# One Transformer layer on one core: the second token block's last products ahead of new weights at two norms, and two of four quads scaled on VectorE

## The chip, the core and the metric

The kernel runs on one core of one Trainium2 chip. The time is the device time of one execution in microseconds (us), the median of several. The engines are named as in the profile: PE is TensorE's matrix multiplication and PEld its weight load, DVE is VectorE, ACT is ScalarE, POOL is GpSimd and SP is SyncE, whose queue issues most loads. All of them work at once, each in the order of its own queue, and wait for one another by semaphores.

## What is computed

One decoder layer for 256 tokens of width 2048 in float32: a half-step SwiGLU feed-forward network (ffn 1), a norm, a mixer of two attention branches, a norm, a second feed-forward network (ffn 2) and a last norm. Cut to what matters here:

```python
def _layer_norm(x, g, b):
    mu = jnp.mean(xf, axis=-1, keepdims=True)
    var = jnp.mean(jnp.square(xf - mu), axis=-1, keepdims=True)
    return (xf - mu) * lax.rsqrt(var + LN_EPS) * g + b

def _swiglu(x, w_gate, w_up, w_down):
    return (jax.nn.silu(x @ w_gate) * (x @ w_up)) @ w_down

h = _layer_norm(ALPHA * h + 0.5 * _swiglu(h, ffn1...), ln1_g, ln1_b)
mix = _mixer(h, ...)          # starts with h @ w_in, ends with y @ w_out
h = _layer_norm(ALPHA * h + mix, ln2_g, ln2_b)
h = _layer_norm(ALPHA * h + 0.5 * _swiglu(h, ffn2...), ln3_g, ln3_b)
```

The two norms in the middle, ln1 and ln2, are the "inner" ones: each needs whole rows of what was just multiplied, and everything after it needs its result.

## The kernel before

**Precision.** Each float32 operand is held as two fp32r tiles, a rounded one and the rest: `split` (L151) casts on ScalarE (L152, the high part) and subtracts on VectorE (L153, the low part). `triple` (L204) then makes three matmuls of 512 columns out of one product (L205 to L207). Weights are loaded by SP into `raw` buffers (four of them), split into one of a ring of pairs (`wring`), and used. The activations are held the same way in `Acts`, as 16 tiles of 128 channels in four quads for each of two token blocks of 128 tokens. `Acts.put` (L137) splits one quad; `made[q, b]` is that quad's subtraction on VectorE.

**Order.** Work is traced in units. One unit is 256 rows of a weight: a load, a split (`prep`), the products of the first token block and those of the second. `project` (L209) goes over the units of one weight matrix. With a lag, the products of the second block are kept in the deque `behind` and run only when more than `lag[0]` units wait there (`catch_up`, L166). Around the inner norms `widen` (L926) sets the lag to 5 and the ring to 10 pairs. So at the end of a stage the first block's products end five units ahead of the second's; the first block's norm is to be computed while the second's products still run, and the second block's while the next weights meet the first block. In the traced order, the held units of the old stage stand between the first units of the new weights. What is traced is then ordered for each engine at build time, by what is ready and by place in the trace. `tc.issue_after(ins)` adds an order: what its block traces on the engine of `ins` comes behind `ins` in that engine's queue, without waiting for it to end.

**A norm.** `LayerNorm.evac` (L739) adds a finished bank to the residual rows `z` (L749, L751) and takes statistics (L754, L760). With the last bank of a block comes `apply` (L764): aggregate (L766), `rstd` (L657: two small VectorE operations, a root on ScalarE at L661, three small VectorE operations), and then for each of the four quads a scaling of the rows (L784) and `rows_to_quad` (L644). The latter turns 128 x 512 on TensorE by four transposes into one of three `tr` banks (L647), has ScalarE apply the gain and the bias of each channel in four activations of 128 columns (L652), and gives the result to `Acts.put`. Later, `finish` (L788) applies gain and bias to the rows as well (L790, L791), for the next residual, and writes them from POOL's queue (L1322). `later(n, fn)` holds such a step until n more units have run.

**The places.** `ffn` (L796) ends with the down projection in `Sliced.run` and `look(0, 0)` (L918). `mixer` (L1037) begins with `project(a["wc0"], ...)` (L1079), followed by wc1 and wc2 of 256 and 320 columns. After `w_out`, `ffn` 2 begins with `project(wgu[0], ...)` (L857), where `behind_x=3` queues the split's VectorE part of unit 3 and later behind `made[0, 0]`. After that come groups of seven products in place of eight (`Hybrid`, L340), in the mixer for two gate matrices (three groups) and for dq, dk and dv; the flag `small` marks the mixer's. At the end of a group, two additions close the second weight's banks (L450, L451), in the mixer all of them queued behind the newest split traced so far (`behind_split`, L333). `dqT` and `dkT` then go through VectorE, a write and a read of DRAM by POOL's queue, and a copy on ScalarE (L704) before the scores (L1156).

Of the kernel before, what the change touches and what calls it, by code (L numbers as in the profile page):

```python
# [18 lines left out]
P = 128  # L19
# [40 lines left out]
def layer_kernel(ctx: ExitStack, tc: tile.TileContext, a: dict, out: bass.AP):  # L60
# [55 lines left out]
    class Acts:  # L116
        def __init__(self, k, name, kept=()):
            self.name = name
            self.kept = kept
            self.tiles = {}  # L120
            self.ready = set()
            self.made = {}
            self.raws = {}

# [12 lines left out]
        def put(self, q, b, src, i0=0, n=4):  # L137
            hi, lo = self.quad(q, b)
            hi, lo = hi[:, i0:i0 + n, :], lo[:, i0:i0 + n, :]
            if len(src.shape) == 4:  # L140
                hi, lo = (v.rearrange("p k (i c) -> p k i c", i=4) for v in (hi, lo))
            self.made[q, b] = split(hi, lo, src)
            self.ready.update((4 * q + i0 + i, b) for i in range(n))

# [63 lines left out]

    def project(w, x, k_tiles, width, done, k0=0, hook=None, between=None, behind_x=None):  # L209
        banks = [None, None]  # L210
# [14 lines left out]
        def one(j):  # L225
# [8 lines left out]
            def prep():  # L234
                pair = [t[:, :G * width] for t in next_pair()]
                with tc.issue_after(x.made[0, 0].ins) if behind_x is not None and j >= behind_x else nullcontext():
                    for c in parts:
                        split(*(t[:, c] for t in pair), st["raw"][:, c])
                st["pair"] = [t.rearrange("p (g n) -> p g n", g=G) for t in pair]
# [100 lines left out]
    class Hybrid:  # L340
# [14 lines left out]

        def group(self, w0, w1, done, wide=False, seeded=False):
            banks = {}
# [68 lines left out]
            def plain(n, j, last=False):  # L426
# [13 lines left out]
                def now():  # L440
                    wh, wl = st["pair"]
                    for b in range(2):
                        o, first = bank(names[b])
                        for g in range(G):
                            k = 2 * j + g
                            triple(o, self.x.at(0, k, b), self.x.at(1, k, b), wh[:, g, :], wl[:, g, :],
                                   first and g == 0, last and g == 1, n == 1 or seeded)
                    if last:
                        with behind_split(1) if small else nullcontext():
                            done(1, 0, banks["Z"], n2, ALU.add)  # L450
                            done(1, 1, banks["X"], q5, ALU.add)  # L451
# [192 lines left out]
    def rows_to_quad(src, b, x, q, gain=None, shift=None):  # L644
# [3 lines left out]
        if gain is not None:  # L648
            full = x.raw(q, b) if q in x.kept else tmp_tile([P, 512], "full")
            for i in range(4):  # L650
                k = 4 * q + i
                S.activation(full[:, i * P:(i + 1) * P], t[:, i * P:(i + 1) * P], AF.Identity,  # L652
                             bias=shift[:, k:k + 1], scale=gain[:, k:k + 1])
            t = full
        x.put(q, b, t.rearrange("p (i t) -> p i t", i=4))

    def rstd(v, eps, n, between=None):  # L657
        ve = sm(n, "ve")
        V.tensor_scalar(out=ve, in0=v, scalar1=eps, scalar2=None, op0=ALU.add)
        sd = sm(n, "sd")  # L660
        S.activation(sd, ve, AF.Sqrt, scale=4.0)  # L661
        w = sm(n, "w")
# [43 lines left out]
    class LayerNorm:  # L706
        def __init__(self, scale, residual, g, bt, each, x=None, cols=None, at=((0, 2, 4, 6), (8, 11, 14, 17)), root_at=1):
# [11 lines left out]
            self.gb = [[None, None] for _ in range(2)]  # L719
            self.applied = {}  # L720

            def rows(h, b):
# [41 lines left out]
        def apply(self, b):  # L764
# [5 lines left out]
            if self.cols is None:  # L770
# [10 lines left out]
                return  # L781
            r = rstd(mv[:, 1:2], LN_EPS, 1)
            for c in range(4):
# [11 lines left out]

    def ffn(n, x, wgu, wdn, residual, g, bt, each, first=None, between=None, nxt=None, cols=None):  # L796
        hb = {}
# [53 lines left out]
        def first_hook(j):  # L851
            if first is not None:
                first(j)
            if j == 5:
                for i, f in enumerate([extra.make] + seven.steps):
                    later(2 * i + 1 - (i > 0), f)
        project(wgu[0], x, KD, 512, lambda b, bank: gu_done(0, b, bank), hook=first_hook,  # L857
                between=between, behind_x=3 if n == 2 else None)
        project(wgu[1], x, KD, 512, lambda b, bank: gu_done(1, b, bank), hook=second)
        look(3, 4)  # L860
# [21 lines left out]
        for p in range(2):  # L882
# [30 lines left out]
            else:  # L913
# [3 lines left out]
                     lambda m, b, bank, p=p: ln.evac(2 * p + m, b, bank), calls, 8 * p)  # L917
        look(0, 0)  # L918

    def at_unit(u, fn):  # L920
# [115 lines left out]

    def mixer(x):  # L1037
        c_row = [act_tile([P, 1024], F32, "c_row") for _ in range(2)]
# [39 lines left out]

        project(a["wc0"], x, KD, 512, cq_done)  # L1079
        narrow_to(6)  # L1080
# [28 lines left out]
        for i, f in ((0, 0), (1, 0), (0, 2)):  # L1109
            w = (a["wgm"], a["wgd"])[i]  # L1110
            hy.group(w[f], w[f + 1], lambda n, b, bank, snap, op, i=i, f=f: keep_gate(i, f + n, b, bank, snap, op),
                     False, f == 2)

# [210 lines left out]

    h1 = Acts(KD, "h1", (0, 1))
    ffn(1, xq, a["gu1"], a["dn1"], a["x"], a["ln1_g"], a["ln1_b"], keep(0), first_tokens, second_tokens, h1, a["ln1_cols"])

    yq = mixer(h1)
    h2 = Acts(KD, "h2", (0, 1, 2))
    ln = LayerNorm(1.0, res[0], a["ln2_g"], a["ln2_b"], keep(1), h2, a["ln2_cols"])  # L1330
    for c in range(4):
        project(a["w_out"][c], yq, KD, 512, lambda b, bank, c=c: ln.evac(c, b, bank),
                hook=at_unit(0, widen) if c == 3 else None)

    ffn(2, h2, a["gu2"], a["dn2"], res[1], a["ln3_g"], a["ln3_b"],
        lambda b, c, z: nc.sync.dma_start(out[b * P:(b + 1) * P, c * 512:(c + 1) * 512], z))
    catch_up(0)
# [84 lines left out]
```

## Time and profile before

| what | value |
| --- | --- |
| time, median of three runs | 1982.71 us (1981.73 to 1983.70) |
| the profiled execution, time | 1981.89 us |
| its span in the profile | 1979.8 us |
| TensorE's mean granted clock in it | 0.999 of full speed |
| DMA | 484.63 MB, mean 245 GB/s |

The span is the part of the time that the profile covers; 2.1 us lie outside it. Times in the listings are microseconds from the start of the span. A row of the order of time has the start, the time until the end of the last of the instructions merged in it, the engine, the line, what is written and what is read, and in square brackets how long the engine had sat idle before and what ended that. `mm` and `tr` are PSUM banks, `h` the split activations, `y` the mixer's result, `z` a norm's rows. Matmuls overlap, so a row of 0.39 us does not mean that the next can start only then.

### The profile page before, as it was taken

To read this page: it belongs to the slowest core of one execution; us is meant where nothing else is said; L and a number is where in the kernel's file an instruction comes from. 1 tells how busy PE (TensorE), PEld (TensorE's weight loads), DVE (VectorE), ACT (ScalarE), POOL (GpSimd) and SP (SyncE) were. 2 spreads that over 40 slices of the span, in tenths; PEclk is the share of its full clock that TensorE was granted. 3 is DMA by queue.
4 is the path that set the end of the run, shared out by engine and by line. 5 is a ranking of instruction groups with operands and counts; after the bars stand their busy time and mean duration, and the time that the engine had idled before them with its cause. 6 is when DMAs were issued, how large, how long until landed. Compare 5 with 4: busy or idle time off the path is not lost.

```text
span 1979.8 us, 25620 instructions
## 1 busy us (share of the span) xinstructions
PE 1960.8 (99%) x8796; PEld 1621.2 (82%) x8796; DVE 1756.0 (89%) x2135; ACT 1261.4 (64%) x1637; POOL 294.3 (15%) x515
## 2 busy tenths in 40 slices
PE   9999999999999999999999999999999999999997
PEld 7888888888888798888788888878888888888886
DVE  7999999999998889998877676699999999989886
ACT  6666666766655566666667765566676666666552
POOL 0221112112100011002223120012112121121000
PEclk9999999999999999999999999999999999999999
DMA  8978888778777666677667667579888877787763
GB/s 303 292 234 272 273 257 252 226 221 316 252 231 260 216 214 242 220 250 250 219 209 249 232 216 273 183 245 289 240 290 268 243 241 238 214 323 256 245 214 125
DMA packets 144594, 484.63 MB, mean 245 GB/s; under 512 B 20640, under 2 KB 20688, under 8 KB 144464
## 3 DMA queue, kind: packets, MB, share of 16 engines
q1 hardware_dynamic: 112752, 389.60, 57.2%
q0 software_dynamic: 31712, 93.41, 17.7%
q8 instruction: 69, 1.13, 0.2%
q14 instruction: 61, 0.50, 0.1%
HBM read 454.08 MB, written 28.84 MB: 244 GB/s over the span
## 4 chain that ended last, share of the span: by engine, by line
PE 48%; DVE 3%; issue 1%; DMA 1%; ACT 1%; POOL 0%; DVEq 0%; POOLq 0%; ACTq 0%
PE mm L206 15%; PE mm L207 15%; PE mm L205 15%; DVE wring L153 2%; DVE sraw L405 1%; DMA turn<-blocks 1%; PE tr L205 0%; PE tr L207 0%; PE tr L206 0%; POOL turn L684 0%; ACT wring L152 0%; DMA turned<-turn 0%; DVE blocks L682 0%; PE tr L1229 0%; PE tr L1231 0%
## 5 line engine op out<-in xcount | busy, mean ns | idle before, releaser
L152 ACT CAST wring<-raw 128x1024 fp32r<-128x1024 f32 (+2 forms) x475 | 490.6, 1038 | 340.7 <-PE mm L207 249.4
L153 DVE TENSOR_TENSOR wring<-raw,wring 128x1024 fp32r<-128x1024 f32 (+2 forms) x475 | 566.9, 1200 | 121.1 <-ACT wring L152 118.1
L152 ACT CAST wring<-sraw 128x1024 fp32r<-128x1024 f32 x436 | 452.0, 1051 | 191.9 <-DVE sraw L405 76.5
L153 DVE TENSOR_TENSOR wring<-sraw,wring 128x1024 fp32r<-128x1024 f32 x436 | 520.9, 1218 | 26.7 <-ACT wring L152 24.6
L207 PE MATMUL mm<-wring,h 128*128 128x512 f32 (+2 forms) x1260 | 484.7, 385 | 0.0
L206 PE MATMUL mm<-wring,h 128*128 128x512 f32 (+2 forms) x1260 | 484.3, 385 | 0.1
L205 PE MATMUL mm<-wring,h 128*128 128x512 f32 (+2 forms) x1260 | 483.8, 385 | 0.4 <-ACT h L152 0.4
L206 PE MATMUL mm<-wring,xs 128*128 128x512 f32 x776 | 303.1, 391 | 1.8 <-DVE wring L153 1.2
L205 PE MATMUL mm<-wring,xs 128*128 128x512 f32 x776 | 302.3, 390 | 0.0
L207 PE MATMUL mm<-wring,xs 128*128 128x512 f32 x776 | 302.0, 389 | 0.0
L206 PEld LDWEIGHTS mm<-wring,h 128*128 128x128 f32 x1260 | 236.7, 188 | 47.7 <-DVE wring L153 1.4
L205 PEld LDWEIGHTS mm<-wring,h 128*128 128x128 f32 x1260 | 236.7, 188 | 47.4 <-ACT h L152 0.9
L207 PEld LDWEIGHTS mm<-wring,h 128*128 128x128 f32 x1260 | 236.7, 188 | 47.2 <-DVE h L153 0.7
L405 DVE TENSOR_TENSOR sraw<-sraw,sraw 128x1024 f32<-128x1024 f32 x168 | 199.3, 1217 | 3.5 <-DMA sraw<-in_wdv_dram 2.4
L206 PEld LDWEIGHTS mm<-wring,xs 128*128 128x128 f32 x776 | 145.7, 188 | 35.7 <-DVE wring L153 5.6
L205 PEld LDWEIGHTS mm<-wring,xs 128*128 128x128 f32 x776 | 145.7, 188 | 30.3
L207 PEld LDWEIGHTS mm<-wring,xs 128*128 128x128 f32 x776 | 145.7, 188 | 29.8
L206 PE MATMUL mm<-wring,x 128*128 128x512 f32 x348 | 135.9, 390 | 0.7 <-DVE wring L153 0.7
L205 PE MATMUL mm<-wring,x 128*128 128x512 f32 x348 | 135.1, 390 | 0.7 <-ACT wring L152 0.5
L207 PE MATMUL mm<-wring,x 128*128 128x512 f32 x348 | 135.3, 389 | 0.0
L684 POOL DMA_DIRECT2D hT<-blocks x176 | 96.8, 562 | 186.4 <-DVE blocks L682 186.4
L407 POOL DMA_DIRECT2D sraw<-in_gu_dram x40 | 35.5, 887 | 511.7 <-DVE sraw L405 406.2
(301 smaller groups left out, 2210.4 us busy)
## 6 DMA issues: line engine op xcount, KB each, us to landing
raw<-in_gu_dram SPq DMA_DIRECT2D x167, 512.0 KB, 5.1
sraw<-in_gu_dram SPq DMA_DIRECT2D x160, 512.0 KB, 5.3
raw<-in_dn_dram SPq DMA_DIRECT2D x140, 512.0 KB, 4.8
sraw<-in_gu_dram POOLq DMA_DIRECT2D x40, 512.0 KB, 7.0
sraw<-in_dn_dram SPq DMA_DIRECT2D x36, 512.0 KB, 6.2
hraw<-hT POOLq DMA_DIRECT2D x68, 256.0 KB, 5.7
raw<-in_w_out_dram SPq DMA_DIRECT2D x32, 512.0 KB, 4.3
eraw<-in_gu_dram SPq DMA_DIRECT2D x48, 256.0 KB, 5.7
```

The source lines that it names most:

```text
L152: cast[0] = S.copy(hi, src)
L153: return V.tensor_tensor(out=lo, in0=src, in1=hi.bitcast(F32), op=ALU.subtract)
L205: PE.matmul(o, xh, wh, start=first, stop=False, skip_group_check=again)
L206: PE.matmul(o, xh, wl, start=False, stop=False, skip_group_check=again)
L207: PE.matmul(o, xl, wh, start=False, stop=last, skip_group_check=again)
L405: V.tensor_tensor(out=t, in0=t, in1=R[add[1]][s], op=ALU.add)
L407: nc.gpsimd.dma_start(R["12"][s], source("22", s), accum_op=ALU.add)
L684: nc.gpsimd.dma_start(to.rearrange("(g r) (i f) -> i r g f", g=4, i=4)[i], t[32 * i:32 * (i + 1), :].rearrange("r (g f) -> r g f", g=4))
```

## The change

Five edits belong together.

- At the end of `ffn`, and after the last `w_out` projection, `catch_up(0)` traces all held second-block units before anything of the next stage; `ffn` returns its norm.
- `project` takes the norm (`norm`) in place of `behind_x`. It queues the splits of its weight units on both engines: at the first projection those from unit 3 on behind the first quad of the first block (on VectorE `made[0, 0]`; on ScalarE the first block's root for unit 3, that quad's cast for the others), and those from unit 7 on behind the second block's last scaling of rows and its root. The second projection of ffn 2 queues all its splits behind the latter (`free=(0, 0)`). Units 0 to 2 of the first projection stay free. wc0 in the mixer, which had no such order, gets it too.
- `rows_to_quad` scales the odd quads (1 and 3) on VectorE, by one multiplication that reads the bank and one addition, each over 512 columns with the gain or bias broadcast; quads 0 and 2 stay on ScalarE. Quad 3's multiplication is queued behind `made[0, b]`.
- `rstd` hands out the root's instruction, and `Acts` remembers the cast of each quad.
- In the mixer, the two additions at the end of a group are queued behind the newest split in the three gate groups alone, no longer for dq, dk and dv.

```diff
         def put(self, q, b, src, i0=0, n=4):
...
             self.made[q, b] = split(hi, lo, src)
+            self.cast[q, b] = cast[0]
...
-    def project(w, x, k_tiles, width, done, k0=0, hook=None, between=None, behind_x=None):
+    def project(w, x, k_tiles, width, done, k0=0, hook=None, between=None, norm=None, free=(3, 7)):
...
                 pair = [t[:, :G * width] for t in next_pair()]
-                with tc.issue_after(x.made[0, 0].ins) if behind_x is not None and j >= behind_x else nullcontext():
+                waits = ()
+                if norm is not None and j >= free[0]:
+                    if j >= free[1]:
+                        waits = norm.applied[1], norm.root[1]
+                    else:
+                        waits = norm.x.made[0, 0], norm.root[0] if j == free[0] else norm.x.cast[0, 0]
+                with ExitStack() as stack:
+                    for i in waits:
+                        stack.enter_context(tc.issue_after(i.ins))
                     for c in parts:
                         split(*(t[:, c] for t in pair), st["raw"][:, c])
...
-        def group(self, w0, w1, done, wide=False, seeded=False):
+        def group(self, w0, w1, done, wide=False, seeded=False, gates=False):
...
                     if last:
-                        with behind_split(1) if small else nullcontext():
+                        with behind_split(1) if gates else nullcontext():
                             done(1, 0, banks["Z"], n2, ALU.add)
                             done(1, 1, banks["X"], q5, ALU.add)
...
     def rows_to_quad(src, b, x, q, gain=None, shift=None):
...
-            for i in range(4):
-                k = 4 * q + i
-                S.activation(full[:, i * P:(i + 1) * P], t[:, i * P:(i + 1) * P], AF.Identity,
-                             bias=shift[:, k:k + 1], scale=gain[:, k:k + 1])
+            if q % 2 == 1:
+                v, o = (u.rearrange("p (i t) -> p i t", i=4) for u in (full, t))
+                g, b0 = (u[:, 4 * q:4 * q + 4].unsqueeze(2).to_broadcast([P, 4, P]) for u in (gain, shift))
+                with tc.issue_after(x.made[q - 3, b].ins) if q > 2 else nullcontext():
+                    V.tensor_tensor(out=v, in0=o, in1=g, op=ALU.mult)
+                V.tensor_tensor(out=v, in0=v, in1=b0, op=ALU.add)
+            else:
+                for i in range(4):
+                    k = 4 * q + i
+                    S.activation(full[:, i * P:(i + 1) * P], t[:, i * P:(i + 1) * P], AF.Identity,
+                                 bias=shift[:, k:k + 1], scale=gain[:, k:k + 1])
...
-    def rstd(v, eps, n, between=None):
+    def rstd(v, eps, n, between=None, root=None):
...
-        S.activation(sd, ve, AF.Sqrt, scale=4.0)
+        sqrt = S.activation(sd, ve, AF.Sqrt, scale=4.0)
+        if root is not None:
+            root.append(sqrt)
...
-            r = rstd(mv[:, 1:2], LN_EPS, 1)
+            r = rstd(mv[:, 1:2], LN_EPS, 1, None, self.root)
...
         project(wgu[0], x, KD, 512, lambda b, bank: gu_done(0, b, bank), hook=first_hook,
-                between=between, behind_x=3 if n == 2 else None)
-        project(wgu[1], x, KD, 512, lambda b, bank: gu_done(1, b, bank), hook=second)
+                between=between, norm=norm)
+        project(wgu[1], x, KD, 512, lambda b, bank: gu_done(1, b, bank), hook=second, norm=norm, free=(0, 0))
...
         look(0, 0)
+        catch_up(0)
+        return ln
...
-        project(a["wc0"], x, KD, 512, cq_done)
+        project(a["wc0"], x, KD, 512, cq_done, norm=norm)
...
             hy.group(w[f], w[f + 1], lambda n, b, bank, snap, op, i=i, f=f: keep_gate(i, f + n, b, bank, snap, op),
-                     False, f == 2)
+                     False, f == 2, True)
...
-    ffn(1, xq, a["gu1"], a["dn1"], a["x"], a["ln1_g"], a["ln1_b"], keep(0), first_tokens, second_tokens, h1, a["ln1_cols"])
+    ln1 = ffn(1, xq, a["gu1"], a["dn1"], a["x"], a["ln1_g"], a["ln1_b"], keep(0), first_tokens, second_tokens, h1, a["ln1_cols"])
...
-    yq = mixer(h1)
+    yq = mixer(h1, ln1)
...
                 hook=at_unit(0, widen) if c == 3 else None)
+    catch_up(0)
...
-        lambda b, c, z: nc.sync.dma_start(out[b * P:(b + 1) * P, c * 512:(c + 1) * 512], z))
+        lambda b, c, z: nc.sync.dma_start(out[b * P:(b + 1) * P, c * 512:(c + 1) * 512], z), norm=ln)
```

More of the change, by code (lines that the diff above doesn't have):

```diff
@@ L122, in __init__ @@
             self.made = {}
+            self.cast = {}
             self.raws = {}
@@ L720, in __init__ @@
             self.applied = {}
+            self.root = []
             def rows(h, b):
@@ L794, in apply, with ffn @@
                 later(12 + c, lambda c=c: finish(c))
-    def ffn(n, x, wgu, wdn, residual, g, bt, each, first=None, between=None, nxt=None, cols=None):
+    def ffn(n, x, wgu, wdn, residual, g, bt, each, first=None, between=None, nxt=None, cols=None, norm=None):
         hb = {}
@@ L1035, in p_cols, with mixer @@
         return pt
-    def mixer(x):
+    def mixer(x, norm):
         c_row = [act_tile([P, 1024], F32, "c_row") for _ in range(2)]
```

## The prediction

> **What bounds the kernel now.** I read the page first, then who TensorE waited for, then the order of time of TensorE and VectorE around both inner norms.
>
> ```profile
> span 1979.8 us, 25620 instructions
> ## 1 busy us (share of the span) xinstructions
> PE 1960.8 (99%) x8796; PEld 1621.2 (82%) x8796; DVE 1756.0 (89%) x2135; ACT 1261.4 (64%) x1637; POOL 294.3 (15%) x515
> ```
>
> TensorE is the bound, and 99% says that little waiting is left to take away. The view of waits, for TensorE alone between 20 and 1960 us, names nearly all of it (columns: us in total, times, longest):
>
> ```profile
> PE mm L206 <- DVE wring L153: 1.2, 3, 0.7
> PE tr L1156 <- ACT dkT L704: 1.0, 1, 1.0
> PE tr L647 <- DVE z L784: 0.9, 2, 0.5
> PE tr L647 <- ACT h1raw L652: 0.7, 1, 0.7
> PE tr L647 <- ACT h2raw L652: 0.7, 1, 0.7
> PE mm L205 <- ACT h L152: 0.4, 2, 0.2
> ```
>
> Four of the six rows are the norms (0.9 + 0.7 + 0.7 + 0.4 = 2.7 us), two lie in the mixer or nearly so (2.2 us). These are idle times after a matmul's modelled end; what a wait costs is larger, since matmuls overlap, so I take it from starts. The first norm (end of ffn 1), on TensorE:
>
> ```profile
> 688.32 0.39 PE L207 MATMUL mm<-wring,h 128*128 128x512 f32 x1
> 689.19 1.50 PE L647 MATMUL tr<-ident,z 128*128 128x128 f32 x12 [0.48 <-DVE z L784]
> 691.41 0.66 PE L647 MATMUL tr<-ident,z 128*128 128x128 f32 x4 [0.73 <-ACT h1raw L652]
> 692.27 0.50 PE L205 MATMUL mm<-wring,h 128*128 128x512 f32 x1 [0.20 <-ACT h L152]
> ```
>
> At 688.32 the last old product starts; the old second-block products have therefore already run ahead here, and nothing is left to cover the first block's norm. Why that norm is late stands on VectorE:
>
> ```profile
> 682.90 0.26 DVE L766 BATCH_NORM_AGGREGATE mv<-bn 128x2 f32<-128x24 f32 x1
> 683.08 1.18 DVE L153 TENSOR_TENSOR wring<-raw,wring 128x1024 fp32r<-128x1024 f32 x1
> ...
> 688.50 1.91 DVE L784 TENSOR_SCALAR z<-z,mv,f 128x512 f32<-128x512 f32 x4
> ```
>
> Between the statistics (682.90) and the normalised rows (688.50) splits of new weights got in, the first of which is shown. The second norm (ln2) looks different:
>
> ```profile
> 1277.67 0.39 PE L206 MATMUL mm<-wring,y 128*128 128x512 f32 x1
> 1278.13 1.54 PE L647 MATMUL tr<-ident,z 128*128 128x128 f32 x12
> 1279.42 0.48 PE L207 MATMUL mm<-wring,y 128*128 128x512 f32 x1
> ...
> 1291.23 0.39 PE L207 MATMUL mm<-wring,y 128*128 128x512 f32 x1
> ...
> 1295.31 0.39 PE L207 MATMUL mm<-wring,h 128*128 128x512 f32 x1
> 1296.08 1.57 PE L647 MATMUL tr<-ident,z 128*128 128x128 f32 x12 [0.38 <-DVE z L784]
> 1298.33 0.66 PE L647 MATMUL tr<-ident,z 128*128 128x128 f32 x4 [0.69 <-ACT h2raw L652]
> 1299.19 0.50 PE L205 MATMUL mm<-wring,h 128*128 128x512 f32 x1 [0.20 <-ACT h L152]
> ```
>
> Here old products (y) are spread among new ones (h) up to 1291.23, so the second block's norm starts late and runs out of cover at 1295.31. The first block's norm is hidden: behind its 12 transposes an old product follows at once.
>
> **Unit prices.** Products start 0.225 us apart (the last window below: 178 in 40.00 us). Hidden transposes take (1279.42 - 1278.13) / 12 = 0.108 us each, 16 of them 1.73 us, and switching into a group costs (1278.13 - 1277.67) - 0.225 = 0.23 us.
>
> **Term 1, the first norm.** From 688.32 to 692.27 are 3.95 us; less one product (0.225) and 16 transposes (1.73) that have to run anyway, 2.0 us are lost. Lines with `norm` queue the splits from the fourth weight unit on behind the first finished quad on VectorE, and on ScalarE behind the root or that quad's cast. What the chain takes without splits, ln2 shows:
>
> ```profile
> 1275.70 0.26 DVE L766 BATCH_NORM_AGGREGATE mv<-bn 128x2 f32<-128x24 f32 x1
> ...
> 1277.43 1.92 DVE L784 TENSOR_SCALAR z<-z,mv,f 128x512 f32<-128x512 f32 x4
> ```
>
> 1.73 us instead of 688.50 - 682.90 = 5.60. The rows would be normalised at 684.63, and with the same 3.77 us from there to a first new product (692.27 - 688.50) that product is possible at 688.4. TensorE has old products until 688.32 + 0.225 = 688.55 and the 16 transposes among them until 690.3. So the whole loss goes, and two switches of at most 0.23 stay or are halved: I take **-1.8** (bounds -1.5 to -2.0, for two switches and none).
>
> **Term 2, the second norm.** From 1295.31 to 1299.19 are 3.88 us; less 0.225 and 1.73, 1.92 are lost. `catch_up(0)` puts the five held units of the second block ahead of new weights: with them go 30 products, the second block's addition, statistics, root, four scalings of rows, 16 transposes and its splits, but no DMA (the block's four writes on POOL's queue come with `finish`, which falls due five units earlier, since `catch_up` counts no steps). So many y products are among the new ones (the windows view, of the instructions that touch y alone):
>
> ```profile
> 1282.00:1291.50 9.50, 3.03 (x12) 2.07 (x11) 0.00 (x0) 0.00 (x0) 1.00 0.69 216
> ```
>
> Run first, the twelve take 2.7 us and the last starts near 1284.5. The chain from the last y to a second-block product is 1299.19 - 1291.23 = 7.96 us, so such a product is possible at 1292.5, while 48 first-block products (10.8 us) and the transposes (1.73) keep TensorE until 1297.2. Two switches stay: **-1.6** (bounds -1.4 to -1.9). If this cover went, 7.96 us would lie open.
>
> **Term 3, quads on VectorE.** Of each norm 2 blocks x 2 quads leave ScalarE (4 activations each) and become a multiply and an addition on VectorE; the price of one:
>
> ```profile
> 700.23 1.29 DVE L790 TENSOR_TENSOR z<-z,gb 128x512 f32<-128x512 f32 x2
> ```
>
> ```profile
> L790 DVE TENSOR_TENSOR z<-z,gb 128x512 f32<-128x512 f32 x8 | 5.2, 687 | 0.0
> ```
>
> A pair ends after 1.29 us and one lasts 0.687, so the second starts 0.60 us after the first, and 8 x 0.60 = 4.8 us a norm, 9.6 in all, are added on VectorE. Reading a bank and a broadcast operand isn't shown in one instruction; the pair of L1100 under term 4, which reads a bank (mm), takes 1.28, so I take 0.60, with the whole 0.687 as the other end (11.0 us in all).
> [...]
> Whether VectorE has room, windows tell (us; busy of PE, PEld, DVE, ACT, POOL with counts; clock; DMA share; GB/s):
>
> ```profile
> 680.00:700.00 20.00, 18.59 (x90) 14.71 (x89) 16.32 (x33) 12.60 (x27) 0.01 (x1) 1.00 0.41 130
> 700.00:740.00 40.00, 39.97 (x257) 36.97 (x256) 35.27 (x63) 27.42 (x52) 8.69 (x16) 1.00 0.70 240
> 1280.00:1300.00 20.00, 18.73 (x90) 14.59 (x89) 17.37 (x28) 14.12 (x31) 0.26 (x1) 1.00 0.56 185
> 1300.00:1340.00 40.00, 40.00 (x178) 33.11 (x177) 38.94 (x52) 26.73 (x39) 5.87 (x10) 1.00 0.74 253
> ```
>
> VectorE is idle 3.7 us in the first and 4.7 in the second: 8.4 against 4.8. At ln2 it is 2.6 + 1.1 from 1280 to 1340, less than 4.8. What gives way is `finish` (16 operations of 0.60), for which nothing on TensorE waits. The splits of units 3 to 7 now come behind the norm (the one at 683.08 after 688); the loads behind them on SP's queue wait for their raw buffers, but DMA is at 0.41 there. If a split is late, TensorE waits about one split, 1.18 us (the row at 683.08), at each norm, unless second-block products fill in. Between 0 and 2.36 I take **+0.2**, near 0, because those products are ready by then.
>
> **Term 4, the mixer.** In the dq, dk and dv groups the two last additions no longer queue behind the newest split:
>
> ```profile
> 947.86 0.39 PE L207 MATMUL mm<-wring,h 128*128 128x512 f32 x1
> ...
> 953.67 1.28 DVE L1100 TENSOR_TENSOR dkTr<-mm,snap 128x512 f32<-128x512 f32 x2
> ```
>
> The banks were complete soon after 947.86; the additions came 5.4 us later. They may now come that early, in front of splits instead of behind: same work, another order. It adds nothing; bounds are -2.2 (both mixer rows of the waits) and +3.6 (three groups x two additions x 0.60, each just ahead of a split that TensorE waits for). The wait on dkT is for the copy of a bank's first rows, which this doesn't touch, so I take **0**.
>
> **Sum.** -1.8 - 1.6 + 0.2 + 0 = -3.2. The profiled execution took 1981.89 (span 1979.8 and 2.1 around it), 0.8 under the median of 1982.71; it would become 1978.7, and the median **1979.5**.
>
> **Rivals.** (a) The mixer's waits go too: -5.4, **1977.3**. For it: the wait on wring at the start of the dv group stands in the very stretch that the additions leave. Against: only the order changes, no work leaves VectorE. (b) Late splits: the norms' gaps come back as waits for wring, one split at each, plus the switches: -3.4 + 2.36, **1981.7**. For it: units 3 to 7 all queue behind the norm and VectorE has 5 splits, 8 scalings and the second norm to do within 12.5 us of TensorE work (10.8 + 1.73). Against: x is ready early, and any ready half unit can run. (c) Slower: VectorE becomes the bound. The added 9.6 us lie open where it is already full (1300 to 1340 above all, and at the first norm under the narrow weights wc1 and wc2, which give TensorE half the columns per split or a little more), giving 1982.7 - 3.4 + 9.6 = **1988.9**. It loses to the old kernel as soon as more than 3.4 of the 9.6 are uncovered, and by over 0.2% from 7.4. Against it: no row of TensorE's waits names a split in these stretches today. (d) The order doesn't change, since the old products already run first at ln1: then only the splits' order works, -1.8, inside (b)'s range.
>
> **How the numbers follow.** Forecast 45%, with its own range 1978 to 1981; (a) 23%; (b) with (d) 17%; (c) 15%. 0.2%, about what a measurement of this kernel can tell from no change, is 4.0 us, so faster means under 1978.7: all of (a) and 16 of the forecast's 45, 0.39; same 0.46; slower 0.15. The range leaves out most of (c) and the tail of (a): 1976.8 to 1985.5.
>
> **What would show it.** In the profile after: at the first norm no wring between the aggregate and L784, and old products or transposes up to the first new one without an idle mark; at ln2 no y product after the first h, and the second block's 12 transposes between h products; L647's rows gone from TensorE's waits; ScalarE's activations at the norms halved, two VectorE rows of 8 on `full`/`h1raw`/`h2raw`. Wrong would be: wring rows of several us in TensorE's waits right behind the norms ((b), (c)), or a changed total in 940 to 1150 larger than at the norms.

## The result, and the profile after

| | before | after |
|---|---|---|
| median of runs, us | 1981.73 (7 runs, 1980.13 to 1983.7) | 1988.0 (7 runs, 1987.05 to 1989.08) |
| profiled execution, us (span) | 1981.89 (1979.8) | 1987.59 (1985.7) |
| ratio after / before | | 1.0031, 95% interval 1.002 to 1.0043 |

The changed kernel is slower by about 6 us. The prediction was 1979.5 with a range to 1985.5, so both miss. What came is close to rival (c), VectorE as the bound, at 1988.9, and the waits below show the sign that the prediction named for (b) and (c): rows of several us for split weights.

The page of after:

```profile
span 1985.7 us, 25563 instructions
## 1 busy us (share of the span) xinstructions
PE 1963.6 (99%) x8796; PEld 1621.7 (82%) x8796; DVE 1764.5 (89%) x2151; ACT 1250.5 (63%) x1605; POOL 294.5 (15%) x515
```

VectorE has 16 instructions and 8.5 us more, ScalarE 32 instructions and 10.9 us less, TensorE the same 8796 matmuls. The page looks like a fair trade: VectorE at 89% seems to have 220 us to spare. The view of waits, TensorE alone between 20 and 1966 us (us in total, times, longest), says otherwise:

```profile
PE mm L208 <- DVE wring L155: 5.7, 8, 1.3
PE mm L207 <- ACT wring L154: 3.2, 1, 3.2
PE tr L657 <- DVE z L804: 0.3, 2, 0.2
```

Of the six rows before (4.9 us), those of the norms are gone but for 0.3 us, the dkT row too; in their place TensorE waits 8.9 us for split weights (wring). L154 and L155 are the split's cast and subtraction, L207 to L209 the three products of a split, L657 the transposes, L804 the scaling of rows: 152, 153, 205 to 207, 647 and 784 before.

**At the norms the change does what it says.** First norm, VectorE, in order of time:

```profile
681.20 0.26 DVE L786 BATCH_NORM_AGGREGATE mv<-bn 128x2 f32<-128x24 f32 x1
...
682.57 1.92 DVE L804 TENSOR_SCALAR z<-z,mv,f 128x512 f32<-128x512 f32 x4
```

From statistics to scaled rows 1.37 us instead of 5.60, with no split between. TensorE at the same place:

```profile
682.72 0.39 PE L209 MATMUL mm<-wring,h 128*128 128x512 f32 x1
683.27 1.50 PE L657 MATMUL tr<-ident,z 128*128 128x128 f32 x12 [0.16 <-DVE z L804]
684.52 0.48 PE L207 MATMUL mm<-wring,h 128*128 128x512 f32 x1
```

684.52 - 682.72 = 1.80 us, less one product (0.225) and 12 transposes (12 x 0.108 = 1.30), leaves 0.28 us lost; by the same working the last four transposes, three products later, lose 0.17 (starts 685.07 and 685.90). Before, 2.0 us were lost. At the second norm:

```profile
1285.30 0.39 PE L209 MATMUL mm<-wring,y 128*128 128x512 f32 x1
1285.53 0.39 PE L207 MATMUL mm<-wring,h 128*128 128x512 f32 x1
...
1293.69 0.39 PE L207 MATMUL mm<-wring,h 128*128 128x512 f32 x1
1293.96 1.52 PE L657 MATMUL tr<-ident,z 128*128 128x128 f32 x12
1295.24 0.48 PE L208 MATMUL mm<-wring,h 128*128 128x512 f32 x1
```

The last y product starts at 1285.30 and not at 1291.23; new h products follow it at once, and the second block's transposes stand between h products with no idle mark. 1295.24 - 1293.69 - 0.225 - 1.30 leaves 0.03 us.

**Where it is lost.** For this the start of the k-th matmul of after is set against the k-th of before, with the difference at 100 us taken off (plus is late, in us). The columns are times in the kernel before. It is worked out from all matmul records of one execution each; single executions of these kernels scatter by 1 to 2 us round their medians, by 3 us in e2_finish_late and e8_double, and a few lie further off (one of e4_quads_finish at 1987.77, 9.0 over its median). The rows named e1 to e12 are the experiments of the next section.

```
before at us        660    690    715    740    800    930    970   1150   1270   1300   1330   1360   1600
after               0.0   -1.2   -1.6    1.2    3.4    3.4    1.6    1.8    1.8    0.1    0.1    6.9    6.9
e1_quads_act        0.0   -1.2   -1.5   -1.6    0.6    0.6   -1.5    0.4    0.4   -1.2   -0.7   -0.7   -0.7
e2_finish_late      0.0   -1.2   -1.5    0.6    2.8    2.8    0.5    0.6    0.6   -1.1   -1.1    3.7    3.8
e3_mixer_only       0.0    0.0    0.0    0.0    1.1    1.1    0.3    0.8    0.8    0.8    0.8    0.8    0.8
e4_quads_finish     0.0   -1.2   -1.6   -1.6    0.1    0.1   -2.2   -2.1   -2.1   -3.8   -3.4   -3.4   -3.4
e5_quads_ln1        0.0   -1.2   -1.6    1.2    4.5    4.5    3.4    3.4    3.5    1.8    2.2    2.2    2.2
e6_quads_ln2        0.1   -1.1   -1.5   -1.2    0.7    0.7   -0.9    0.1    0.1   -1.6   -1.5    4.8    4.8
e7_quads_block0     0.0   -1.2   -1.6   -0.0    2.3    2.3   -0.0    0.1    0.1   -1.6   -1.6   -1.5   -1.5
e8_double           0.0   -1.2    1.7    6.0    7.8    7.8    5.5    5.5    5.5    6.5    8.8   17.9   17.9
e9_no_catch_up      0.0   -1.2   -0.2   -0.2    2.0    2.0   -0.0    2.1    2.1    1.9    2.0    2.8    2.8
e10_wc0_free        0.0    0.0    0.0    0.0   -0.5   -0.5   -2.0   -1.9   -1.9   -3.7   -3.4   -3.4   -3.3
e11_no_mixer_edit   0.0   -1.2   -1.6   -1.6    0.9    0.9   -0.1   -0.1   -0.1   -1.9   -1.5   -1.5   -1.4
e12_finish_20       0.0   -1.2   -1.6   -1.6   -1.0   -1.0   -2.4   -2.3   -2.3   -3.9   -3.8   -3.8   -3.7
```

The row of after reads from left to right: 1.6 us won at the first norm, 2.8 lost from 715 to 740 and 2.2 more to 800; 1.8 won in the mixer (930 to 970); 1.7 won at the second norm (1270 to 1300); 6.8 lost from 1330 to 1360. The large loss stands some 40 us and more behind the second norm. VectorE's sraw additions (L415, 405 before) and POOL's accumulating loads (L417, 407 before) of ffn 2's halved weights lead there. After, in order of time on four engines:

```profile
1332.42 2.35 DVE L415 TENSOR_TENSOR sraw<-sraw,sraw 128x1024 f32<-128x1024 f32 x2
...
1334.20 0.89 POOL L417 DMA_DIRECT2D sraw<-in_gu_dram  x1 [5.73 <-PE mm L209]
...
1343.20 1.04 ACT L154 CAST wring<-sraw 128x1024 fp32r<-128x1024 f32 x1 [3.93 <-DMA sraw<-in_gu_dram]
...
1342.15 0.39 PE L209 MATMUL mm<-wring,h 128*128 128x512 f32 x1
1345.73 0.51 PE L207 MATMUL mm<-wring,xs 128*128 128x512 f32 x1 [3.19 <-ACT wring L154]
1346.99 0.50 PE L208 MATMUL mm<-wring,xs 128*128 128x512 f32 x1 [0.75 <-DVE wring L155]
```

The same places before:

```profile
1328.14 2.36 DVE L405 TENSOR_TENSOR sraw<-sraw,sraw 128x1024 f32<-128x1024 f32 x2
...
1329.92 0.89 POOL L407 DMA_DIRECT2D sraw<-in_gu_dram  x1 [4.64 <-PE mm L207]
```

VectorE comes to the additions 4.3 us later (4.8 us had been added to its queue), the loads are issued 4.3 us later, ScalarE waits 3.93 for one, TensorE 3.19 + 0.75 for the split. The view of the chain that ended last, from 1318 to 1352 in after, ties these together (start, length):

```profile
1332.50 1.70 DVE sraw L415 x2
1334.20 8.91 DMA sraw<-in_gu_dram
1343.20 1.04 ACT wring L154
```

Ahead of these rows the chain runs mostly through VectorE's splits and `finish`, behind them through the split to TensorE; in before it holds nothing but matmuls in that window. Why the 4.8 found no room shows in one row of the windows from 1290 to 1340 (us; busy of PE, PEld, DVE, ACT, POOL with counts; clock; DMA share; GB/s), first before, then after:

```profile
1290.00:1340.00 50.00, 48.73 (x222) 39.84 (x221) 48.12 (x70) 31.32 (x50) 6.13 (x10) 1.00 0.72 244
```

```profile
1290.00:1340.00 50.00, 50.00 (x227) 40.54 (x227) 48.77 (x72) 28.80 (x41) 6.08 (x10) 1.00 0.73 248
```

VectorE was already idle for only 1.9 of 50 us, and ScalarE, from which the work was taken, for 18.7. A full window is not a loss by itself: e1 below, with all quads on ScalarE, is busy for 49.13 of these 50 us and loses no more than 0.5 there (-1.2 to -0.7 in the table). It means that work put ahead of the window or into it makes everything behind it late. By this reading TensorE loses once the splits and loads held in stock are used up.

### The profile page after: what moved, and what is told of

The parts are those of the page before. It is cut to its first block, busy times and chain, and to the rows that moved or that the text cites. A ratio compares the mean times of both kernels' runs of the same rounds, so it can differ in the third digit from the quotient of the medians.

```text
span 1985.7 us, 25563 instructions
## 1 busy us (share of the span) xinstructions
PE 1963.6 (99%) x8796; PEld 1621.7 (82%) x8796; DVE 1764.5 (89%) x2151; ACT 1250.5 (63%) x1605; POOL 294.5 (15%) x515
## 4 chain that ended last, share of the span: by engine, by line
PE 83%; DVE 10%; issue 2%; DMA 2%; ACT 2%; SPq 0%; DVEq 0%; ACTq 0%
PE mm L208 26%; PE mm L209 26%; PE mm L207 26%; DVE wring L155 5%; DVE sraw L415 2%; ACT wring L154 1%; PE tr L207 1%; PE tr L209 1%; PE tr L208 1%; DVE blocks L701 1%; DMA sraw<-in_wdk_dram 1%; DMA sraw<-in_gu_dram 0%; PE tr L657 0%; DVE z L811 0%; DVE z L810 0%
## 5 line engine op out<-in xcount | busy, mean ns | idle before, releaser
L154 ACT CAST wring<-raw 128x1024 fp32r<-128x1024 f32 (+2 forms) x475 | 491.1, 1038 | 341.9 <-PE mm L209 240.4
L155 DVE TENSOR_TENSOR wring<-raw,wring 128x1024 fp32r<-128x1024 f32 (+2 forms) x475 | 567.8, 1201 | 110.0 <-ACT wring L154 107.2
L154 ACT CAST wring<-sraw 128x1024 fp32r<-128x1024 f32 x436 | 451.4, 1052 | 195.7 <-DVE sraw L415 77.4
L155 DVE TENSOR_TENSOR wring<-sraw,wring 128x1024 fp32r<-128x1024 f32 x436 | 521.4, 1220 | 37.3 <-ACT wring L154 35.6
L209 PE MATMUL mm<-wring,h 128*128 128x512 f32 (+2 forms) x1260 | 484.9, 385 | 0.0
L207 PE MATMUL mm<-wring,h 128*128 128x512 f32 (+2 forms) x1260 | 483.1, 385 | 0.0
L207 PE MATMUL mm<-wring,xs 128*128 128x512 f32 x776 | 302.8, 390 | 3.2 <-ACT wring L154 3.2
L209 PE MATMUL mm<-wring,xs 128*128 128x512 f32 x776 | 302.4, 390 | 0.0
L207 PEld LDWEIGHTS mm<-wring,h 128*128 128x128 f32 x1260 | 236.6, 188 | 46.8 <-ACT h L154 0.7
L209 PEld LDWEIGHTS mm<-wring,h 128*128 128x128 f32 x1260 | 236.7, 188 | 46.5 <-DVE h L155 0.2
L415 DVE TENSOR_TENSOR sraw<-sraw,sraw 128x1024 f32<-128x1024 f32 x168 | 199.3, 1219 | 2.9 <-DMA sraw<-in_wdv_dram 1.9
L207 PEld LDWEIGHTS mm<-wring,xs 128*128 128x128 f32 x776 | 145.9, 188 | 34.7 <-ACT wring L154 4.5
L209 PEld LDWEIGHTS mm<-wring,xs 128*128 128x128 f32 x776 | 146.0, 188 | 30.1
L209 PE MATMUL mm<-wring,x 128*128 128x512 f32 x348 | 135.4, 390 | 0.0
L207 PE MATMUL mm<-wring,x 128*128 128x512 f32 x348 | 134.9, 390 | 0.0
L417 POOL DMA_DIRECT2D sraw<-in_gu_dram x40 | 35.5, 887 | 508.8 <-DVE sraw L415 498.2
```

The source lines that it names most:

```text
L154: cast[0] = S.copy(hi, src)
L155: return V.tensor_tensor(out=lo, in0=src, in1=hi.bitcast(F32), op=ALU.subtract)
L207: PE.matmul(o, xh, wh, start=first, stop=False, skip_group_check=again)
L209: PE.matmul(o, xl, wh, start=False, stop=last, skip_group_check=again)
L415: V.tensor_tensor(out=t, in0=t, in1=R[add[1]][s], op=ALU.add)
L417: nc.gpsimd.dma_start(R["12"][s], source("22", s), accum_op=ALU.add)
```

## The experiments

Two theories first. **Theory 1**: the quads' scaling on VectorE (9.6 us of added work) is the cost, and the rest of the change gains what was forecast. **Theory 2**: it is `finish` (L810, L811), which since `catch_up` falls due five units earlier and crowds the splits. The first two kernels below apply one remedy each. The third is the mixer's edit alone, put into the kernel before; the fourth has both remedies.

**All quads back on ScalarE** (edit to after):

```diff
-            if q % 2 == 1:
+            if q % 2 == 2:
```

> The changed kernel with all four quads scaled by ScalarE again; the rest of the change stays. Theory 1 (the 4.8 us of added VectorE work at each norm make the splits late): VectorE's queue behind ln2 gets back 4.8 us, the wait of 3.2 us for the cast of sraw near 1342 us goes, so do the waits at 723 to 755; 1988 falls to about 1979. Theory 2 (finish of the second block falls due four units earlier and stands in front of the splits): these waits stay, since finish is as early as before; 1986 to 1988.

Measured: median 1978.77 (11 runs), ratio to before 0.9982 (0.9974 to 0.9991). Theory 1 holds: the quads' move cost 1988.0 - 1978.77 = 9.2 us, and the rest of the change gains 3.2 (the kernel before, run beside it, took 1981.95). What TensorE waits for in it from 20 to 1966:

```profile
PE mm L208 <- DVE wring L155: 2.4, 3, 1.0
PE tr L1198 <- ACT pt L1056: 0.8, 1, 0.8
PE tr L1218 <- DVE orow L1211: 0.6, 1, 0.6
PE tr L657 <- DVE z L804: 0.3, 2, 0.2
```

No wait on ScalarE's wring is left, and in the table the loss from 1330 to 1360 is 0.0 instead of 6.8. This kernel and after differ in the quads alone, and VectorE comes to the sraw additions 5.1 us earlier than in after (1332.42); the accumulating load is early again:

```profile
1327.35 1.23 DVE L415 TENSOR_TENSOR sraw<-sraw,sraw 128x1024 f32<-128x1024 f32 x1
...
1329.23 0.89 POOL L417 DMA_DIRECT2D sraw<-in_gu_dram  x1 [5.49 <-PE mm L209]
```

**`finish` of the second block due later** (edit to after):

```diff
-                later(12 + c, lambda c=c: finish(c))
+                later(12 + 4 * b + c, lambda c=c: finish(c))
```

> The changed kernel with finish of the second block due four units later, as in the kernel before; the quads stay on VectorE. Theory 1: the added 4.8 us are still there and still in front of the splits, so most of the waits stay, 1985 to 1988. Theory 2: the waits at 723 to 755 and at 1342 go, about 1980.

Measured: 1987.61 (8 runs, 1984.5 to 1990.77), ratio 1.0027 (1.0017 to 1.0038). Theory 2 falls: the due time alone gives nothing that can be told from after. Its profiled execution (1985.48, 2.1 under its median) adds something about the stall behind the second norm. The waits of TensorE from 1260 to 1400, and POOL:

```profile
PE mm L207 <- ACT wring L154: 2.0, 1, 2.0
PE mm L208 <- DVE wring L155: 0.8, 1, 0.8
```

```profile
1329.77 0.90 POOL L417 DMA_DIRECT2D sraw<-in_gu_dram  x1 [3.13 <-PE mm L209]
```

Here the load is issued as early as before (1329.77 against 1329.92), and TensorE still waits 2.8 us and falls 4.8 us behind from 1330 to 1360. So the late load is the form that the loss takes in after, and not its only form: with `finish` moved back, finish operations stand between later splits and sraw additions instead.

**The mixer's edit alone** (in the kernel before):

```diff
-                        with behind_split(1) if small else nullcontext():
+                        with behind_split(1) if gates else nullcontext():
...
```

The lines left out hand the flag `gates` to the three gate groups, as in the change.

> The kernel before with one edit alone: the additions at the end of a group are queued behind the newest split only in the gate groups. If the edit is what took TensorE's waits at 950.7 and 962.1 (1.9 us of starts) out of the changed kernel, this one is 1.9 us faster than before, about 1980. If those waits went because the norms moved the mixer in time, it stays within 0.5 us of before.

Measured: 1980.64, ratio 0.9992 (0.9983 to 1.0001): 1.3 us in its favour by the medians, not clear of zero, and between the two values expected.

**Both remedies**, e1's and e2's edits:

> Both: all quads on ScalarE and finish four units later, so of the change the order at the norms and the mixer's additions are left. If the two together are the whole loss, the waits behind both norms are gone and the gains stay (1.6 and 1.7 at the norms, 1.9 in the mixer): 1976 to 1978. If the order at the norms loses something by itself (all splits of the second projection behind the second norm), it stays above 1980.

Measured: 1978.74, ratio 0.9984 (0.9974 to 0.9994), the same as e1 and a little above the 1976 to 1978 expected if all gains added up.

Next, **how** the quads cost 9.2 us: everywhere at the same price, or only where VectorE has nothing idle? The condition is limited to one norm, then to the first block; one kernel adds 9.6 us more (the bias subtracted and added again, twice eight pairs).

```diff
-            if q % 2 == 1:
+            if q % 2 == 1 and x.name == "h1":
```

> The changed kernel with quads 1 and 3 on VectorE at ln1 alone; at ln2 ScalarE scales all four. Theory (what VectorE is given at a norm is lost there, each norm for itself): the waits of the changed kernel at 712 to 740 stay (2.8 us of starts), those at 1315 to 1420 go (6.7 us): 1978.8 + 2.8, about 1981.6. Rival (the two norms are not independent, the loss at ln2 is due to the order downstream of ln1): above 1985.

```diff
-            if q % 2 == 1:
+            if q % 2 == 1 and x.name == "h2":
```

> Quads 1 and 3 on VectorE at ln2 alone. Theory: 1978.8 + 6.7, about 1985.5, with the wait for the cast of sraw (3.2 us) near 1340 us and a lower granted clock right behind it. Rival: under 1981.

```diff
-            if q % 2 == 1:
+            if q % 2 == 1 and b == 0:
```

> The changed kernel with quads 1 and 3 on VectorE for the first token block alone, at both norms: half the added work (2.4 us a norm), put where VectorE waits for ScalarE anyway (in the kernel before 2.4 us idle before the first quad's subtraction at ln2). Theory A (the amount counts, VectorE's queue is late by what is added): about half the loss, 1983 to 1984. Theory B (only work in the full stretch counts): nearly no loss, 1979 to 1980.

```diff
                 V.tensor_tensor(out=v, in0=v, in1=b0, op=ALU.add)
+                V.tensor_tensor(out=v, in0=v, in1=b0, op=ALU.subtract)
+                V.tensor_tensor(out=v, in0=v, in1=b0, op=ALU.add)
```

> The changed kernel with two more VectorE operations of 128x512 for each quad on VectorE (the bias taken off and added again; the result is the same but for rounding), so 4.8 us more of VectorE work at each norm. If the stretch behind each norm is bound by VectorE, each added us is lost: 1988 + 9.2, about 1997. If the loss was one wait that lets the rest in behind it, it grows by less than half of that, under 1992.

| kernel | VectorE work added to e1, us | median, us | over e1, us | ratio to before (95%) |
|---|---|---|---|---|
| e7, first block of both norms | 4.8 | 1979.67 | 0.9 | 0.999 (0.9981 to 0.9999) |
| e5, first norm | 4.8 | 1981.72 | 2.9 | 0.9995 (0.9986 to 1.0004) |
| e6, second norm | 4.8 | 1984.89 | 6.1 | 1.0015 (1.0006 to 1.0024) |
| after, both | 9.6 | 1988.0 | 9.2 | 1.0031 (1.002 to 1.0043) |
| e8, both, twice | 19.2 | 2001.67 | 22.9 | 1.0095 (1.0081 to 1.0108) |

The two norms add up (2.9 + 6.1 = 9.0 of 9.2). The same 4.8 us of work cost 0.9, 2.9 or 6.1 us according to where they stand. The first block's share is nearly free. At the second norm it runs in the windows row of after from 1262 to 1285, where VectorE is busy for 13.32 of 23 us:

```profile
1262.00:1285.00 23.00, 22.85 (x108) 18.53 (x108) 13.32 (x25) 8.86 (x16) 0.00 (x0) 1.00 0.33 112
```

The second block's share joins the queue of 1290 to 1340, without a gap, and makes up nearly all of the cost. What TensorE waits for says which place: in e6 from 1260 to 1400, and in e7 from 20 to 1966,

```profile
PE mm L207 <- ACT wring L154: 2.8, 2, 2.6
PE mm L208 <- DVE wring L155: 0.8, 1, 0.8
```

```profile
PE mm L208 <- DVE wring L155: 3.0, 3, 1.4
```

and in e8, of which from 20 to 1980 stand

```profile
PE mm L208 <- DVE wring L155: 9.5, 10, 2.1
PE mm L207 <- ACT wring L154: 5.9, 2, 5.6
```

The wait for ScalarE's cast has grown to 5.6 us, and 9.6 us of work more than in after lengthen the run by 13.7 by the medians (four runs of e8, 1998.57 to 2002.53) and by 11.0 in the table, whose execution is the fastest of the four. Both are more than the 9.2 expected; what makes the second portion dearer than the first wasn't followed up.

Then the parts that **gain**, each taken out of e1: `catch_up(0)` at both norms; the split order at wc0; the mixer's edit.

```diff
-        catch_up(0)
         return ln
...
-    catch_up(0)
```

> All quads on ScalarE as in e1_quads_act, and catch_up(0) taken out at both norms; the orders of the splits stay. If the second norm's gain (1.7 us of starts at 1290 to 1300) comes from the old products run first, it goes: 1978.8 + 1.7, about 1980.5, with y products among the new ones again. At the first norm nothing changes, since the old products ran first there before the change. Rival (the order of the splits alone does it): 1978.8.

```diff
-        project(a["wc0"], x, KD, 512, cq_done, norm=norm)
+        project(a["wc0"], x, KD, 512, cq_done)
```

> All quads on ScalarE, catch_up(0) in place, but wc0's splits without the order behind the first norm. Theory (the first norm's gain of 1.6 us is given back by 800 us, where the gate groups wait for splits anyway: in e4_quads_finish TensorE was 2.7 us ahead of the kernel before at 740 and 1.0 at 800, 1.1 at the start): the gap of 2 us at the first norm is back and the waits at 740 to 800 shrink by as much, the time stays within 0.7 us of 1978.8. Rival (the gain lasts): 1980.4.

```diff
-                        with behind_split(1) if gates else nullcontext():
+                        with behind_split(1) if small else nullcontext():
```

> All quads on ScalarE, the order at the norms as changed, the mixer's additions queued behind the newest split in all groups as before. If the mixer's edit is worth what e3_mixer_only showed (1.3 us), this is 1978.8 + 1.3, about 1980.1; if the waits at 950 and 962 depend on where the norms leave the mixer, anything from 1978.8 to 1982.

**e9**, without `catch_up`: 1982.38, ratio 1.0008 (0.9999 to 1.0016). The expectation missed: it costs 3.6 us against e1 where 1.7 were expected, and not at the second norm alone. Two of its rows of waits from 20 to 1966:

```profile
PE tr L657 <- ACT h1raw L669: 0.7, 1, 0.7
PE tr L657 <- ACT h2raw L669: 0.7, 1, 0.7
```

The first norm waits as in before (h1raw); in the table only 0.2 us of its 1.6 are won by 715, although the splits wait for the norm.

**e10**, without the split order at wc0: 1978.69, ratio 0.9985 (0.9977 to 0.9994), the same as e1. TensorE from 660 to 860:

```profile
PE tr L657 <- ACT h1raw L669: 0.7, 1, 0.7
PE tr L657 <- DVE z L804: 0.5, 1, 0.5
PE mm L207 <- ACT h L154: 0.2, 1, 0.2
```

The gap at the first norm is all back, with `catch_up` in place (0.0 at 715), and the run is no longer: the waits for wring that e1 has from 740 to 800 (2.4 us) are gone with it. What the first norm wins is lost again within 100 us.

**e11**, without the mixer's edit: 1979.36, ratio 0.999 (0.9981 to 0.9999), 0.6 more than e1 by the medians; the intervals overlap.

Last, from e10's reading: if the splits after the first norm are late because `finish` shares their queue, spreading all finish operations later should keep the gain. Edit to e1:

```diff
-                later(12 + c, lambda c=c: finish(c))
+                later(20 + 2 * c, lambda c=c: finish(c))
```

> All quads on ScalarE, and finish of both blocks due from 20 units on, two units apart, in place of 12 on, one apart: its 9.6 us of VectorE work at each norm come later and thinner. If the remaining waits at 740 to 800 come from VectorE's work behind the first norm, this is faster than e1_quads_act, 1977 to 1978.5; if they come from loads or from the groups' own additions, it is 1978.8 or, with finish now inside the groups, up to 1981.

Measured: 1977.82 (1976.44 to 1978.24), ratio 0.9978 (0.9969 to 0.9987). TensorE from 660 to 860:

```profile
PE mm L208 <- DVE wring L155: 0.8, 2, 0.5
PE tr L657 <- DVE z L804: 0.2, 1, 0.2
```

The waits for wring fall from 2.4 to 0.8 us, and at 800 TensorE is 1.0 us ahead instead of 0.6 late. This version beats both kernels; that it beats e1 by its 1.0 us is not clear, as the intervals overlap.

## Why the prediction was wrong

**The step that failed is term 3**, "between 0 and 2.36 I take +0.2". It measured 9.2 us (after against e1). Its price was right: 0.60 us an operation (in after two multiplications of L664 start at 686.94 and 687.54), 9.6 in all. Its cover was wrong in three ways.

- The room was read as a sum of idle time over 60 us at each norm (8.4 at the first, 3.7 at the second). Cover is idle time in the queue between the place where the work is put and the next split that TensorE lacks. The prediction quoted 38.94 busy of 40 from 1300 to 1340, and the window 1290 to 1340 above shows 48.12 of 50. e5, e6 and e7 show that this place decides: 2.9, 6.1 and 0.9 us for the same work.
- "What gives way is `finish`" was wrong. Its operations stand in VectorE's order among the splits and take their turn there; in after its 16 operations at the second norm were done by 1327.6, ahead of the sraw additions at 1332.42. Even a later due time gave no relief (e2).
- The price of late splits was bounded by one split a norm (2.36 in all), and put near nothing on the ground that second-block products fill in. By the reading above they fill in only until the stock of split units is used up; from there lateness of VectorE's queue reaches TensorE. At the first norm 4.8 us of work cost 2.9. At the second a load and a slow stretch of TensorE (last section) hang on the late additions, and 4.8 us cost 6.1.

Rival (c) had the mechanism, came near in size (9.6 open, 1988.9 against 1988.0 measured) and named the place "1300 to 1340 above all" and the first norm under the narrow weights. It got 15%. That its size fits so well is in part luck: it charged 4.8 a norm, and 2.9 and 6.1 came, the second with 1.7 us of slow clock that it didn't have. The argument against it, that no wait of TensorE named a split there, only told that the stock of splits was not yet empty, not how far it was from it.

**Term 1**, -1.8 at the first norm: 1.6 there by the table, but its cause was half told. The prediction gave the split order all of it, since the old products ran first there before the change. e10 (`catch_up` without the order) shows 0.0 at 715 and e9 (the order without `catch_up`) 0.2: only both together win. And it doesn't last: in e1 the gain is used up by 800, and e10 is as fast without it. What the prediction lacked is that a stretch bound by VectorE follows at once.

**Term 2**, -1.6 at the second norm: 1.7 by the table in after, 1.6 in e1, and in e1 nothing behind the norm takes it back. `catch_up` as a whole is worth 3.6 (e9): against e1 the table of e9 has 1.7 of it by 1270, 1.4 at the second norm and 0.8 from 1330 to 1360. As e10 loses nothing by giving up the first norm's gain, what the first 1.7 is stays open.

**Term 4**, 0 for the mixer: the sign was a gain, its size is open. 1.3 us by e3, 0.6 by e11, neither clear of zero. In the table e1 wins 2.1 from 930 to 970 and e11, without the edit, 1.0. Rival (a)'s 2.2 is reached in the table's stretch by e2, e4 and e7 (2.3 each), but e11 wins 1.0 there without the edit, and no difference of medians reaches it.

**The sum without term 3**, -3.4, agrees with e1's -3.2, but not term by term: the first norm's part was mostly lost again and the mixer's not forecast. e1, e6 and e9 also fall back 1 to 2 us from 970 to 1150 in the table, which e4, e10, e11 and e12 don't; e1's waits at L1198 and L1218 lie there. Those of e6 (L1218) and e9 (L1197 and L1217, the same lines there) do too. What causes them stays open.

## What to carry to other kernels

An engine's idle share is no cover for work added to it: look at its queue from the place where the work is put to the next thing that the bound engine needs from it, and if it has no gap there, expect a large part of the work to be paid, or more than all of it where a load hangs on its end (here 2.9 and 6.1 us for 4.8). Moving work off a less busy engine (ScalarE, 31.32 of 50 us busy from 1290 to 1340) onto one whose local queue is full (VectorE, 48.12) cost 6.1 us here (e6) although no wait in that stretch named that engine before. A gain just ahead of a stretch with another bound is lost again unless that bound is relieved too, as e10 and e12 show at the first norm (at 800 TensorE is 0.6 us late in e1, 0.5 ahead in e10 and 1.0 in e12).

## What the runs showed of the hardware

**Behind the waits at 1342 to 1347 TensorE's granted clock was 0.50 for 3.4 us.** The windows of after, behind the wait of 3.19 us that ends at 1345.73 and the one of 0.75 that ends at 1346.99 (the clock is the third figure from the end):

```profile
1347.00:1348.00 1.00, 1.00 (x4) 0.81 (x5) 0.56 (x1) 1.00 (x2) 0.14 (x1) 0.83 0.97 385
1348.00:1350.00 2.00, 2.00 (x6) 1.05 (x4) 1.09 (x1) 2.00 (x3) 2.00 (x4) 0.50 0.48 121
1350.00:1351.00 1.00, 1.00 (x4) 0.71 (x3) 1.00 (x3) 0.77 (x1) 0.10 (x1) 0.50 0.69 131
1351.00:1352.00 1.00, 1.00 (x6) 0.58 (x4) 1.00 (x2) 0.00 (x0) 0.95 (x2) 0.97 0.01 0
```

The granted clock falls to 0.50 and is back by 1351; worked out from the four rows, it was 0.50 for 3.4 us (0.34 + 2 + 1 + 0.06). TensorE's products there, in order of time:

```profile
1347.89 0.63 PE L208 MATMUL mm<-wring,xs 128*128 128x512 f32 x1
...
1351.16 0.39 PE L207 MATMUL mm<-wring,xs 128*128 128x512 f32 x1
```

From the one start to the other are 3.27 us and seven distances, which at the 0.225 measured at a clock of 1.00 take 1.6: so 1.7 us are lost in the slow stretch, as 3.4 us at 0.50 give too. The first two waits cost 1345.73 - 1342.15 - 0.225 = 3.4 and 1346.99 - 1345.73 - 0.225 = 1.0; with them that is 6.1 of the 6.8 lost from 1330 to 1360. A quarter of the stall stands in no row of waits. From 1340 to 1365 the clock is 0.93 in after and 1.00 in before. In e2 and e6 it is 0.50 from 1347 to 1348, in e8 0.88 from 1340 to 1360; with after these are the four kernels that scale the second block's quads on VectorE at the second norm. In e1, with all quads on ScalarE and no wait for a split there, it is 1.00 from 1347 to 1352. Behind the first norm in after, where the longest wait is 1.29 us (until 756.68), it is 1.00 from 740 to 760. What sets the fall off can't be told from these runs. In e2 the waits were shorter than in after: TensorE waited 1.96 us, ran one product and waited 0.76, and the clock was 0.50 all the same:

```profile
1348.00:1350.00 2.00, 2.00 (x7) 1.52 (x6) 2.00 (x3) 0.63 (x2) 1.86 (x4) 0.50 0.51 86
```

**A bank and a broadcast operand cost VectorE nothing extra here.** The new operations in after, by line and shape (busy us, mean ns of one):

```profile
L664 DVE TENSOR_TENSOR h1raw<-tr,cols 128x512 f32<-128x512 f32 x2 | 1.4, 682 | 0.0
L665 DVE TENSOR_TENSOR h1raw<-h1raw,cols 128x512 f32<-128x512 f32 x2 | 1.4, 683 | 0.0
```

The multiplication reads a bank (tr) and a broadcast gain in 682 ns, the addition from SBUF 683; `finish`'s multiplication of two SBUF operands without a broadcast (L810) takes 684. The other groups of the two lines, on full and h2raw, take 684 to 688.
